# Gate projections of an encoder layer as seven block products instead of eight

## The chip, the cores and the metric

One core of one Trainium2 chip runs the whole layer in one launch. The metric is the device time of that launch in microseconds. Engines are named as in the profile: PE (matrix products), PEld (its weight loads), DVE (VectorE), ACT (ScalarE), POOL (GpSimd) and SP (SyncE, which only issues transfers here). PE writes its results to PSUM, in banks of 128 x 512 float32; everything else on chip lies in SBUF rooms ("tiles" out of pools of a fixed number of rooms).

## The reference

One residual layer over x of 1024 tokens x 1024 channels, float32:

```
h = rmsnorm(x, g_mix);  z = h @ w_in               # pool channels | q | k | v
y_pool = pool_mixer(z[:, :512])                    # trailing windows 2, 4, 8, 16, a map per group
y_attn = diff_attention(q, k, v)                   # 8 heads, two softmax maps each
gates  = sigmoid(h @ w_gate + b_gate)              # w_gate is 1024 x 2048
merged = gates[:, :1024] * (y_pool @ w_branch_pool) + gates[:, 1024:] * (y_attn @ w_branch_attn)
x = x + merged @ w_out
x = x + square(relu(rmsnorm(x, g_ffn) @ w_up)) @ w_down
```

The change concerns `h @ w_gate + b_gate` alone.

## The kernel before

Each float32 factor of a product is kept as two rounded digits, hi and lo, and a product of two factors is three matmuls in one PSUM bank, hi·hi, hi·lo and lo·hi (`mm3`, lines 126 to 128). Making digits is `split`: ACT casts src to hi (line 120), and DVE or POOL subtracts, lo = src - hi (line 121). So a 128 x 512 tile of weights costs one ACT and one DVE or POOL instruction before PE can use it.

The activations h stand transposed in `hT`: eight blocks of 128 channels, two halves of 512 tokens (`th`), two digits. Rows of the outputs of gates, pool channels and so on are channels too, so the gates are 16 blocks of 128 channels (`c`) by two token halves.

The order of the work is this. The eight attention heads run first as a software pipeline over (head, 128 tokens): `z` (q, k, v of a head from `hT`), `tk` (transposes), `sc` (scores), `ta` (transposes of the probabilities), `po` (times v). At the end of each head POOL computes one `r` (line 588). All work of the heads comes first in program order, which is priority here: a scheduler writes each engine's order out ahead of time, and what is later in program order fills the gaps. That filling work, in order, is

- the gates: `gate_cols(c)` loads the weights of a channel block in two halves (`fill_w`, rooms `fr`, two of them), makes digits with POOL's subtract (rooms `fw`, four of them), and for each token half issues 24 matmuls into one bank (`fill_proj`), which ACT copies out with the bias (line 730) and stores to `g_dram`. For c under G_Z = 10 the bank is `ps_f`, of which there is one; from 10 on it is in turn two banks of `ps_z`, which the heads' `z` use until they end, and `ps_f`.
- `weight_unit`, four times: POOL makes sums and digits of `w_branch_attn` for a later stage, started after gate steps 2, 4, 6 and 8.
- the pool channels: `pool_group(g)`, four times, 24 matmuls `u` per token half, a chain of sums on DVE, three matmuls `yp`, and a store to `p_dram`. After nine gate steps (G_FIRST) each half of a group is followed by a gate step.

Behind the heads and the gates come `bp` (16 tiles of 12 matmuls, `branch_pool`), in which each bank is multiplied by a gate half (line 210) that `gate_half` has loaded from `g_dram` and put through the sigmoid (line 828); channel blocks 0 to 7 are used here. Then `ba`, the attention's branch, already as seven block products (`ba_step`, 28 steps of 12 matmuls; banks baX and baY); the gate blocks 8 to 15 are used from its second product on. The stage takes 11 rooms of the pool `up` (`ut`) when the heads have left it: two for `t2`, one for `s2`, four for `wa`, four for `wr`. Then `op` (w_out) and the feed-forward part.

## Time and profile before

| | us |
|---|---|
| median of three runs | 1528.98 (1528.79 to 1530.02) |
| the profiled execution, device time | 1529.71 |
| its span in the profile | 1527.6 |
| last `z` matmul starts | 612.7 |
| last gate matmul starts | 696.7 |
| `bp` | 697 to 740.5 |

The page gives busy time by engine, then the span in 40 slices, each digit the busy share in tenths. In a table by stage each row is one stretch of the span: its length, then for each engine the busy us and, as (x...), the instructions; then PE's granted clock, the busy share of the 16 DMA engines, and GB/s. In a group of instructions the two numbers behind the bar are the busy us and the mean ns of one; in an answer on a tile, the three numbers are the least, the median and the greatest duration in ns.

### The profile page before, as it was taken

What the parts mean: (1) busy time and instruction counts of PE and PEld (TensorE: products, weight loads), DVE (VectorE), ACT (ScalarE), POOL (GpSimd) and SP (SyncE); (2) the same over time, 40 slices, a digit from 0 to 9 for tenths busy, and PEclk for the clock granted to TensorE, in tenths of its full rate; (3) what the DMA queues carried; (4) which work ended last, traced back from release to release, by engine and by line L of the source; (5) the groups of instructions that cost most, each with busy time, mean ns of one, the idle gap of its engine ahead of it and who ended that gap; (6) DMA issues with size and microseconds to landing.
All of it is one profiled execution on the core that took longest, in us unless ns stands there. A gap on an engine that the chain in (4) does not pass through costs nothing.

```text
span 1527.6 us, 21675 instructions
## 1 busy us (share of the span) xinstructions
PE 1509.7 (99%) x7441; PEld 1302.0 (85%) x7441; DVE 1048.5 (69%) x2262; ACT 804.7 (53%) x1693; POOL 319.8 (21%) x412
## 2 busy tenths in 40 slices
PE   7999999999999999999999999999999999999998
PEld 6999999999898989888888888888888888888887
DVE  6776668777777777746578559766665668556572
ACT  6665556656565565454464466555555634333331
POOL 6687333335234242312100011000000000000000
PEclk9999999999999999999999999999999999999999
DMA  7253202112112131627365734554433799537750
GB/s 247 100 159 120 76 29 62 51 44 66 43 44 84 49 98 40 223 89 254 120 209 191 248 104 149 169 178 152 148 128 110 274 344 383 170 125 262 228 190 28
DMA packets 171608, 221.07 MB, mean 145 GB/s; under 512 B 10902, under 2 KB 104811, under 8 KB 171499
## 3 DMA queue, kind: packets, MB, share of 16 engines
q1 hardware_dynamic: 154090, 192.39, 38.0%
q10 hardware_dynamic: 17408, 27.30, 4.8%
q8 instruction: 59, 0.97, 0.3%
q14 instruction: 51, 0.41, 0.1%
HBM read 157.76 MB, written 61.90 MB: 144 GB/s over the span
## 4 chain that ended last, share of the span: by engine, by line
PE 95%; DVE 2%; DMA 1%; ACT 1%; SPq 1%; issue 0%; POOL 0%; DVEq 0%
PE z L126 6%; PE z L128 6%; PE z L127 6%; PE Da L126 4%; PE Da L128 4%; PE Da L127 4%; PE g L126 4%; PE g L127 4%; PE g L128 4%; PE Db L126 3%; PE Db L128 3%; PE Db L127 3%; PE X L128 3%; PE X L127 3%; PE X L126 3%; PE sc L484 2%
## 5 line engine op out<-in xcount | busy, mean ns | idle before, releaser
L126 PE MATMUL z<-wqkv,hT 128*128 128x384 f32 x512 | 174.9, 343 | 0.6 <-DVE qn L428 0.4
L128 PE MATMUL z<-wqkv,hT 128*128 128x384 f32 x512 | 173.7, 340 | 0.0
L127 PE MATMUL z<-wqkv,hT 128*128 128x384 f32 x512 | 173.5, 339 | 0.0
L495 ACT ACTIVATE s<-s,nm 128x256 f32<-128x256 f32 (+7 forms) x128 | 99.5, 778 | 46.5 <-DVE nm L487 45.6
L126 PE MATMUL g<-hT,fwgate 128*128 128x512 f32 x256 | 101.1, 395 | 0.1
L127 PE MATMUL g<-hT,fwgate 128*128 128x512 f32 x256 | 100.8, 394 | 0.0
L128 PE MATMUL g<-hT,fwgate 128*128 128x512 f32 x256 | 100.5, 393 | 0.0
L126 PEld LDWEIGHTS z<-wqkv,hT 128*128 128x128 f32 x512 | 96.8, 189 | 3.4 <-DVE qn L428 0.6
L127 PEld LDWEIGHTS z<-wqkv,hT 128*128 128x128 f32 x512 | 96.9, 189 | 3.1 <-POOL wqkv L121 0.2
L235 POOL TENSOR_TENSOR ms<-ms,mhalf 128x4 f32<-128x4 f32 x64 | 65.7, 1027 | 158.3 <-DVE ms L234 135.3
L128 PEld LDWEIGHTS z<-wqkv,hT 128*128 128x128 f32 x512 | 96.5, 189 | 2.5 <-DVE hT L121 0.3
L121 DVE TENSOR_TENSOR AT<-ta,AT 128x256 fp32r<-128x256 f32 (+1 forms) x160 | 62.2, 392 | 32.7 <-ACT AT L120 31.6
L487 DVE CUSTOM_DVE_ANT_0 s<-sc,dist 128x512 f32<-128x512 f32 (+3 forms) x128 | 73.9, 583 | 13.2 <-PE sc L485 12.1
L120 ACT CAST AT<-ta 128x256 fp32r<-128x256 f32 (+1 forms) x160 | 54.5, 347 | 37.9 <-PE ta L527 23.1
L484 PE MATMUL sc<-K,Q 128*128 128x512 f32 (+2 forms) x192 | 69.8, 365 | 0.5 <-DVE nm L487 0.5
L121 DVE TENSOR_TENSOR AS<-s,AS 128x512 fp32r<-128x512 f32 x64 | 44.1, 693 | 36.5 <-ACT AS L120 36.3
L485 PE MATMUL sc<-K,Q 128*128 128x512 f32 (+2 forms) x192 | 66.4, 350 | 0.0
L121 POOL TENSOR_TENSOR wqkv<-rqkv,wqkv 128x384 fp32r<-128x384 f32 x60 | 61.8, 1044 | 19.8 <-ACT wqkv L120 16.7
L121 POOL TENSOR_TENSOR fwgate<-frgate,fwgate 128x512 fp32r<-128x512 f32 x32 | 43.3, 1356 | 66.0 <-ACT fwgate L120 66.0
L126 PEld LDWEIGHTS g<-hT,fwgate 128*128 128x128 f32 x256 | 48.1, 188 | 9.3 <-ACT go L730 0.5
L128 PEld LDWEIGHTS g<-hT,fwgate 128*128 128x128 f32 x256 | 48.1, 188 | 8.9
L127 PEld LDWEIGHTS g<-hT,fwgate 128*128 128x128 f32 x256 | 48.1, 188 | 8.4
(455 smaller groups left out, 4485.0 us busy)
## 6 DMA issues: line engine op xcount, KB each, us to landing
wd<-in_w_down_dram SPq DMA_DIRECT2D x56, 512.0 KB, 5.6
wu<-in_w_up_dram SPq DMA_DIRECT2D x32, 512.0 KB, 4.4
udS<-us SPq DMA_DIRECT2D x64, 256.0 KB, 2.4
ur<-udS SPq DMA_DIRECT2D x32, 512.0 KB, 3.4
rqkv<-in_w_in_dram SPq DMA_DIRECT2D x64, 192.0 KB, 2.7
ud<-u ACTq DMA_DIRECT2D x48, 256.0 KB, 4.1
ur<-ud SPq DMA_DIRECT2D x24, 512.0 KB, 4.3
frgate<-in_w_gate_dram SPq DMA_DIRECT2D x32, 256.0 KB, 2.8
```

The lines of the kernel that those rows point to most:

```text
L120: nc.scalar.copy(hi, src)
L121: return (lo_eng or nc.vector).tensor_tensor(lo, src, f(hi), op=ALU.subtract)
L126: nc.tensor.matmul(ps, lhs_hi, rhs_hi, start=first, stop=False, **kw)
L127: nc.tensor.matmul(ps, lhs_hi, rhs_lo, start=False, stop=False, **kw)
L128: nc.tensor.matmul(ps, lhs_lo, rhs_hi, start=False, stop=last, **kw)
L235: nc.gpsimd.tensor_tensor(dst, dst, mhalf[:, :n], op=ALU.pow)
L484: nc.tensor.matmul(dst, Q[:, i, 0, :], rhs, start=True, stop=False)
L485: nc.tensor.matmul(dst, Q[:, i, 1, :], rhs, start=False, stop=True)
L487: nc.vector.tensor_tensor_reduce(out=s[i][:, c : c + w], in0=sc[:, 0:w], in1=dist[:, o0 + c : o0 + c + w], scale=2.0 ** -(h + 1), scalar=B ...
L495: nc.scalar.activation(s[i][:, 0:n], s[i][:, 0:n], AF.Exp, bias=last, scale=-1.0, accum_out=Z[:, i, t : t + 1])
```

## The change

With h^T as 2 x 2 blocks (upper and lower 512 input channels, first and second 512 tokens) and w_gate's columns taken in eight groups q of two neighbouring channel blocks, the eight block products of a group become seven (Strassen's scheme in Winograd's form). Each block product is 12 matmuls, so a group issues 84 where it issued 96. Four of the seven need a sum of weight blocks, and four a sum of blocks of `hT`, called T. T takes four 128-channel pieces of two digits: two `fw` rooms, the `fu` room and the `mx` room. It is made four times in turn, in place: t1, t2, t4, t3. Each product or pair of products in one bank is written to a new DRAM tensor `gm_dram` (`spill`), and `sum_gates(q)` reads six of them back into three `ut` rooms, adds five times on POOL, and stores three quarters of the result to `g_dram`; the fourth quarter goes there straight from `first_gate`.

`combine` and the lo subtract are POOL's, except between `late.append(True)` and `late.clear()`, where they are DVE's, weights' digits lie in `wt` rooms (those of the heads' weights), raw weights alternate between the pools `raw` and `fr`, and their loads are issued behind the last load of the heads' weights.

```diff
-PREP_AT = (2, 4, 6, 8)
...
-G_FIRST, G_Z = 9, 10
+G_FIRST = 4
...
-    def gate_cols(c):
-        ws = fill_w(w_gate, c * P, f"gate{c}")
-        for th in range(2):
-            ps = fill_proj(ws, th, f"g{c}_{th}", spare_bank if c >= G_Z else fill_bank)
-            fo = fo_tile(f"go{c}_{th}")
-            nc.scalar.activation(fo[:, 0:512], ps, AF.Identity, bias=cols[:, c : c + 1])
-            nc.scalar.dma_start(g_dram[c * P : (c + 1) * P, th * 512 : (th + 1) * 512], fo[:, 0:512])
-            yield
-
-    def gates():
-        for c in range(2 * NK - 2):
-            yield from gate_cols(c)
-        for gen in [gate_cols(c) for c in (2 * NK - 2, 2 * NK - 1)] * 2:
-            next(gen)
-            yield
+    gm_dram = dram.tile([NK * P, 6 * 512], F32, name="gm_dram")
+    T = {}
+
+    def spill(ps, q, slot, name, m=None, scale=1.0):
+
+        fo = fo_tile(name)
+        if m is None:
+            nc.scalar.copy(fo[:, 0:512], ps)
+        else:
+            c = 2 * q + m
+            nc.scalar.activation(fo[:, 0:512], ps, AF.Identity, bias=cols[:, c : c + 1], scale=scale)
+        if slot is None:
+            dst = g_dram[2 * q * P : (2 * q + 1) * P, 0:512]
+        else:
+            dst = gm_dram[q * P : (q + 1) * P, slot * 512 : (slot + 1) * 512]
+        nc.scalar.dma_start(dst, fo[:, 0:512])
+
+    def raw_gate(dst, q, kh, m):
+        c0 = (2 * q + m) * P
+        nc.sync.dma_start(
+            dst, w_gate[kh * 512 : (kh + 1) * 512, c0 : c0 + P].rearrange("(kk p) c -> p kk c", p=P)
+        )
+
+    def raw_one(q, kh, m, name):
+        if not late:
+            rw = fr_tile([P, 4, P], name)
+            raw_gate(rw, q, kh, m)
+            return rw
+        nraw[0] += 1
+        rw = raw([P, 4, P], name) if nraw[0] % 2 else fr_tile([P, 4, P], name)
+        with tc.issue_after(loaded["wqkv"]):
+            raw_gate(rw, q, kh, m)
+        return rw
+
+    late = []
+    nraw = [0]
+
+    def combine(out, a, b_, op):
+        (nc.vector if late else nc.gpsimd).tensor_tensor(out, a, b_, op=op)
+
+    def digits_of(src, name):
+        w = (wt if late else fw_tile)([P, 2, 4, P], name)
+        stored["lo"] = split(w[:, 0], w[:, 1], src, None if late else nc.gpsimd).ins
+        return w
+
+    def hd(kt, kh, th):
+
+        k = 4 * kh + kt
+        return [hT[k // 2, th, d][:, k % 2, :] for d in range(2)]
+
+    def td(kt):
+        return [T[kt][:, d, :] for d in range(2)]
+
+    def make_T(kt, a, b_, name):
+
+        if kt not in T:
+            if kt < 2:
+                T[kt] = fw_tile([P, 2, 512], f"T{kt}")
+            elif kt == 2:
+                T[kt] = fu_tile("T2").bitcast(F32R).rearrange("p (a b) -> p a b", a=2)
+            else:
+                T[kt] = fq.tile([P, 2, 512], F32R, tag="mx", name="T3")
+        t = T[kt]
+        d = fo_tile(f"{name}_{kt}")[:, 0:512]
+        combine(d, f(a[0]), f(b_[0]), ALU.subtract)
+        combine(d, d, f(a[1]), ALU.add)
+        combine(d, d, f(b_[1]), ALU.subtract)
+        split(t[:, 0, :], t[:, 1, :], d, None if late else nc.gpsimd)
+
+    def product(ps, w, rhs, more=False):
+
+        for kt in range(4):
+            r_hi, r_lo = rhs(kt)
+            mm3(ps, w[:, 0, kt, :], w[:, 1, kt, :], r_hi, r_lo, not more and kt == 0, kt == 3, more)
+
+    def gate_bank(name, spare):
+        return (spare_bank if spare else fill_bank)(name)
+
+    def first_gate(q, spare=False):
+
+        ws = [digits_of(raw_one(q, j, 0, f"gw{j + 1}_{q}"), f"gw{j + 1}_{q}") for j in range(2)]
+        ps = gate_bank(f"gP1_{q}", spare)
+        product(ps, ws[0], lambda kt: hd(kt, 0, 0))
+        spill(ps, q, 0, f"gs1_{q}")
+        product(ps, ws[1], lambda kt: hd(kt, 1, 0), True)
+        spill(ps, q, None, f"gs2_{q}", 0)
+
+    def second_gate(q, spare=False):
+
+        a21, a22 = raw_one(q, 0, 1, f"gw5_{q}"), raw_one(q, 1, 1, f"gx5_{q}")
+        combine(a22, a22, a21, ALU.add)
+        w5 = digits_of(a22, f"gw5_{q}")
+        a11 = raw_one(q, 0, 0, f"gy5_{q}")
+        combine(a11, a11, a22, ALU.subtract)
+        a12 = raw_one(q, 1, 0, f"gz5_{q}")
+        combine(a12, a12, a11, ALU.add)
+        w3 = digits_of(a12, f"gw3_{q}")
+        ps = gate_bank(f"gP5_{q}", spare)
+        product(ps, w5, td)
+        spill(ps, q, 5, f"gs5_{q}", 1)
+        product(ps, w3, lambda kt: hd(kt, 1, 1), True)
+        spill(ps, q, 2, f"gs3_{q}", 0)
+
+    def third_gate(q, spare=False):
+
+        a21, a22 = raw_one(q, 0, 1, f"gx6_{q}"), raw_one(q, 1, 1, f"gy6_{q}")
+        combine(a22, a22, a21, ALU.add)
+        a11 = raw_one(q, 0, 0, f"gz6_{q}")
+        combine(a22, a22, a11, ALU.subtract)
+        ps = gate_bank(f"gP6_{q}", spare)
+        product(ps, digits_of(a22, f"gw6_{q}"), td)
+        spill(ps, q, 1, f"gs6_{q}")
+
+    def fourth_gate(q, spare=False):
+
+        ps = gate_bank(f"gP4_{q}", spare)
+        product(ps, digits_of(raw_one(q, 1, 1, f"gz4_{q}"), f"gw4_{q}"), td)
+        spill(ps, q, 4, f"gs4_{q}", 1, -1.0)
+
+    def fifth_gate(q, spare=False):
+
+        a11, a21 = raw_one(q, 0, 0, f"gx7_{q}"), raw_one(q, 0, 1, f"gy7_{q}")
+        combine(a21, a11, a21, ALU.subtract)
+        ps = gate_bank(f"gP7_{q}", spare)
+        product(ps, digits_of(a21, f"gw7_{q}"), td)
+        spill(ps, q, 3, f"gs7_{q}")
+
+    def sum_gates(q):
+
+        c0, c1, c2 = (ut([P, 2, 512], F32, f"gc{i}_{q}") for i in range(3))
+        for i, c in enumerate((c0, c1, c2)):
+            nc.sync.dma_start(c, gm_dram[q * P : (q + 1) * P, i * 1024 : (i + 1) * 1024])
+        u_, e6, b53, e7, p4, e5 = (c[:, i, :] for c in (c0, c1, c2) for i in range(2))
+        combine(u_, u_, e6, ALU.add)
+        combine(b53, b53, u_, ALU.add)
+        combine(u_, u_, e7, ALU.add)
+        combine(p4, u_, p4, ALU.add)
+        combine(e5, u_, e5, ALU.add)
+        for m, th, c in ((0, 1, b53), (1, 0, p4), (1, 1, e5)):
+            r0 = (2 * q + m) * P
+            nc.sync.dma_start(g_dram[r0 : r0 + P, th * 512 : (th + 1) * 512], c)
...
-    gate_units = gates()
-    steps = [0]
     units_left = [(kk, ch) for kk in range(2) for ch in range(2)]
-
-    def gate_step():
-        more = next(gate_units, "end") != "end"
-        steps[0] += 1
-        if steps[0] in PREP_AT:
-            prepare_weights()
-        return more
 
     def prepare_weights():
         with tc.issue_after(stored["lo"]):
             weight_unit(w_branch_attn, wa_dram, *units_left.pop(0))
 
-    for _ in range(G_FIRST):
-        gate_step()
+    for q in range(G_FIRST):
+        first_gate(q)
+        prepare_weights()
     for g in range(4):
         for _ in pool_group(g):
-            gate_step()
-    while gate_step():
-        pass
+            pass
+    for kt in range(4):
+        make_T(kt, hd(kt, 0, 1), hd(kt, 0, 0), "t1")
+    for q in range(NK):
+        second_gate(q)
+    for kt in range(4):
+        make_T(kt, hd(kt, 1, 1), td(kt), "t2")
+    for q in range(NK):
+        third_gate(q)
+    late.append(True)
+    first_gate(4, True)
+    first_gate(5, True)
+    for kt in range(4):
+        make_T(kt, td(kt), hd(kt, 1, 0), "t4")
+    for q in range(NK):
+        fourth_gate(q, True)
+    first_gate(6, True)
+    for kt in range(4):
+        make_T(kt, hd(kt, 1, 1), hd(kt, 0, 1), "t3")
+    for q in range(NK):
+        fifth_gate(q, True)
+    first_gate(7, True)
+    late.clear()
+    for q in range(NK):
+        sum_gates(q)
     assert not units_left
 
     vpool = attn.enter_context(tc.tile_pool(name="vpool", bufs=1))
```

6 lines of the change are left out of this document (3 added, 3 removed).

## Prediction

> **What bounds the kernel now.** I read the page first: the busy shares, the slices, the chain of work that ended last.
>
> ```profile
> span 1527.6 us, 21675 instructions
> PE 1509.7 (99%) x7441; PEld 1302.0 (85%) x7441; DVE 1048.5 (69%) x2262; ACT 804.7 (53%) x1693; POOL 319.8 (21%) x412
> ...
> GB/s 247 100 159 120 76 29 62 51 44 66 43 44 84 49 98 40 223 89 254 120 209 191 248 104 149 169 178 152 148 128 110 274 344 383 170 125 262 228 190 28
> ...
> PE 95%; DVE 2%; DMA 1%; ACT 1%; SPq 1%; issue 0%; POOL 0%; DVEq 0%
> ```
>
> PE is busy almost without a gap and is 95% of the chain, so a matmul less is worth its time wherever PE stays fed. The next view is the table by stage: start, heads, tail (heads without `z`, with the last gates), `bp`, first part of `ba`.
>
> ```profile
> core 0: us, PE busy (x) PEld busy (x) DVE busy (x) ACT busy (x) POOL busy (x), PEclk, DMA share, GB/s
> ...
> 138.50:612.80 474.30, 473.21 (x2649) 432.33 (x2648) 358.42 (x1108) 278.43 (x750) 179.65 (x217) 1.00 0.19 60
> 612.80:697.00 84.20, 84.20 (x411) 70.15 (x410) 48.32 (x127) 43.02 (x94) 19.54 (x17) 1.00 0.44 152
> 697.00:740.50 43.50, 43.50 (x194) 35.91 (x193) 30.87 (x45) 18.66 (x31) 9.68 (x4) 1.00 0.74 261
> 740.50:770.00 29.50, 29.50 (x132) 24.43 (x131) 17.02 (x27) 13.19 (x23) 0.00 (x0) 1.00 0.29 93
> ```
>
> PE is full in all four at full clock. In the heads DVE is 76% busy, POOL 38%; in the tail POOL is nearly free; under `bp` DVE is at 71% and the transfers at 261 GB/s. The same table for the gate matmuls alone, and for `bp`:
>
> ```profile
> 138.50:612.80 474.30, 91.74 (x357) 1.00 0.19 60
> 612.80:697.00 84.20, 71.23 (x288) 1.00 0.44 152
> ...
> 697.00:740.50 43.50, 43.50 (x192) 1.00 0.74 261
> ```
>
> 288 gate matmuls fill the tail. `bp` is undisturbed 512-column work: 43.5 / 192 = 0.2266 us a matmul, which is how I price one (the durations near 390 ns overlap).
>
> **The change, part by part.** *PE.* 8 groups x (96 - 84) = 96 matmuls go: 96 x 0.2266 = 21.8 us, if PE stays fed. Nothing is added on PE. By the order written, 384 gate matmuls (first_gate of four groups, second, third) use the one filling bank during the heads, against 480 before, and 288 remain for the tail, as many as before. So the gain has to come from shorter heads.
>
> *Do the heads shorten?* The ends of the heads (POOL's `r`) cut the span into head periods; these are the first, the longest and the two shortest of six, for everything, then their gate matmuls, then `u`:
>
> ```profile
> 138.50:219.10 80.60, 80.45 (x447) 73.06 (x446) 53.62 (x173) 44.50 (x120) 30.07 (x37) 1.00 0.19 60
> 219.10:294.30 75.20, 75.20 (x428) 69.28 (x428) 61.86 (x187) 46.22 (x126) 27.83 (x34) 1.00 0.16 51
> 455.60:538.60 83.00, 82.52 (x461) 75.28 (x460) 65.95 (x198) 48.35 (x130) 34.62 (x45) 1.00 0.19 61
> 538.60:612.30 73.70, 73.25 (x415) 66.91 (x414) 55.22 (x174) 43.28 (x119) 25.82 (x29) 1.00 0.24 77
> ...
> 138.50:219.10 80.60, 23.75 (x93) 1.00 0.19 60
> 219.10:294.30 75.20, 12.27 (x48) 1.00 0.16 51
> 455.60:538.60 83.00, 11.59 (x48) 1.00 0.19 61
> 538.60:612.30 73.70, 18.95 (x72) 1.00 0.24 77
> ...
> 138.50:219.10 80.60, 4.51 (x18) 1.00 0.19 60
> 219.10:294.30 75.20, 7.90 (x30) 1.00 0.16 51
> 455.60:538.60 83.00, 12.61 (x48) 1.00 0.19 61
> ```
>
> With 78, 96 and 72 filling matmuls the last three periods shown are 75.2, 83.0 and 73.7 us: fewer fillers, shorter head, at PE's price or faster. The first, with 111, took only 80.6, and over all six periods (fillers 111, 78, 77, 116, 96, 72) the fitted slope is 0.128 us per matmul. So the early loss is between 0 and 96 x (0.2266 - 0.128) = 9.5 us.
>
> It has three places. The pool groups now follow one another with no gate step between, and `yp` waits for a DVE chain. t2 may only overwrite T when the last second_gate product has read it: 16 POOL instructions, some 21 us with little else to fill. And each head's weights come at its very start, load, ACT, then eight subtracts on POOL:
>
> ```profile
> 225.00 10.33 SPq L309 DMA_DIRECT2D rqkv<-in_w_in_dram  x8
> ...
> L121 POOL TENSOR_TENSOR wqkv<-rqkv,wqkv x60: 1003/1015/1470, 9.1 to 546.5; 128x384 fp32r<-128x384 f32 x60
> ```
>
> On SP the a11 and a12 loads of second_gate wait for POOL's sums, and these eight loads can stand behind them; a sum ahead of a subtract costs 1.3 us. Fillers cover that where there are any. I take 5, the middle, since nothing ranks the six periods.
>
> *POOL in the heads.* Lo subtracts: 32 for weights and 8 for t1 and t2, against 20; sums: 40 of weights and 24 for T. That is 84 more, at
>
> ```profile
> L121 POOL TENSOR_TENSOR fwgate<-frgate,fwgate x32: 1278/1292/2191, 26.1 to 672.7; 128x512 fp32r<-128x512 f32 x32
> ...
> L121 POOL TENSOR_TENSOR wbp<-rbp,wbp x8: 1283/1300/4980, 608.9 to 728.3; 128x512 fp32r<-128x512 f32 x8
> ...
> 723.38 6.68 POOL L121 TENSOR_TENSOR wbp<-rbp,wbp 128x512 fp32r<-128x512 f32 x2 [8.08 <-ACT wbp L120]
> ```
>
> 1.292 us: 109 us on POOL's 180 in 474, so about 61%. The heads' own `ms` and `qn` queue behind them for 1.3 us at a time; two `z` banks cover that. second_gate is a chain of three sums and two subtracts on POOL, 6.5 us, with three rounds of loads of 2.8 us: about 15 us for 24 matmuls, where the heads took 24 fillers in some 20 us. Hidden, just.
>
> *ACT* gains 24 hi casts for weights, 16 for T and 24 copies out:
>
> ```profile
> L730 ACT ACTIVATE go<-g,cols 128x512 f32<-128x512 f32 x32 | 21.9, 688 | 15.1 <-PE g L128 13.6 <-DVE cols L372 1.4
> L120 ACT CAST fwgate<-frgate 128x512 fp32r<-128x512 f32 x32 | 19.8, 618 | 12.1 <-PE g L128 10.9 <-DMA frgate<-in_w_gate_dram 1.0 <-ACT oq L560 0.2
> ...
> L121 POOL TENSOR_TENSOR wbp<-rbp,wbp 128x512 fp32r<-128x512 f32 x8 | 14.8, 1865 | 27.7 <-ACT wbp L120 27.7
> ```
>
> 41 us over the heads and tail, in which it is busy 321 of 558. Hidden; if not, a bank comes free 0.7 us late.
>
> *The tail.* DVE gets 24 lo subtracts of weights, 8 sums for P7 and 2 x 16 instructions for t4 and t3:
>
> ```profile
> L199 DVE SCALAR_TENSOR_TENSOR ry<-ry,gs,rb x8: 1269/1285/1502, 613.6 to 714.9; 128x1024 f32<-128x1024 f32 x8
> L846 DVE TENSOR_TENSOR ry<-ry,ry x4: 666/678/1789, 633.5 to 716.9; 128x512 f32<-128x512 f32 x4
> ...
> L210 DVE TENSOR_TENSOR mp<-bp,g x16: 674/683/692, 700.0 to 740.8; 128x512 f32<-128x512 f32 x16
> ```
>
> 64 x 0.683 = 43.7 us on 48.3 that stand there: 92 us of work in 84. About 10 us of it (six L199, two L846) prepares `ba` and may slip. First_gate of 4 and 5 (48 matmuls, 10.9 us) covers t4's 10.9 us of DVE; first_gate of 6 covers half of t3's. Bounds: 0, if the slipping is free, and 7.8 + 10.9 = 19, if PE waits for the excess and for one T. I take 4: half of the excess, as the slipping work has until `ba`.
>
> *The sums behind it.* P7 of group 0 is followed by 7 x 12 + 24 matmuls, 24.5 us. Copy out (0.7), store (2.0), read (4.8) come first, so POOL starts about 17 us ahead of `bp`.
>
> ```profile
> frgate<-in_w_gate_dram SPq DMA_DIRECT2D x32, 256.0 KB, 2.8
> g_dram<-go ACTq DMA_DIRECT2D x32, 256.0 KB, 2.0
> g<-g_dram SPq DMA_DIRECT2D x32, 256.0 KB, 4.2
> ...
> wr<-in_w_branch_attn_dram SPq DMA_DIRECT2D x4, 512.0 KB, 4.8
> ```
>
> The gate halves themselves are in time: `bp` needs a group every 10.9 us, and eight banks let PE run ahead. The rooms are tighter. The sums hold three of eleven `ut` rooms at a time, and `t2`, `s2`, `wa`, `wr` want all eleven; the fourth step of `ba` (51.7 us after `bp` begins) needs `wr` 3, hence its room 6 us before: 63 us after POOL starts. POOL has six other subtracts there. With groups 0 to 5 out of the way (36 instructions) at the 1.865 us that `wbp` averaged (row above): 67 us, 4.5 us late. Bounds: at 1.292 nothing; all 46 at 1.865, 86 us, 23 late. I take 4.5, since the last groups are needed late and `wr` 6 and 7 can wait.
>
> Transfers there: 12.6 MB read and 6.3 MB stored by the sums. Up to 65 us behind `bp`'s start, groups 0 to 5 move 14.2 MB beside some 16.7 MB of old traffic (the stage rows: 152 x 22, 261 x 43.5, 93 x 21.5): 31 MB in 87 us, 355 GB/s, against 383 in the best slice. Full, but not over.
>
> POOL's pace is the weak point: one `wbp` took 4.98 us against 1.28, at 723 to 728, while DVE ran sums of two SBUF tiles without a pause. [...]
>
> *Sum.* -21.8 + 5 + 4 + 4.5 = -8.3 on the profiled execution's 1529.7 (its span is 1527.6, 2.1 lie around it): 1521.4. The median of the runs is 0.7 lower: 1521 rounded.
>
> **The rivals.** *All hidden.* Heads at PE's pace, DVE's excess slipping, sums at 1.3 us: 1529 - 21.8 = 1507. For it: PE has 18 us of gaps in all now (1527.6 less 1509.7). Against: three resources near full at once.
>
> *The sums hold up `ba`* (the other side). POOL at `wbp`'s mean over all 46 instructions, and rooms given to the sums first: PE waits 23 us for `wr` 3; with 5 and 4, 1529 - 21.8 + 32 = 1539. It decides from a mean of 63 / 46 = 1.36 us if all eight groups come first, 1.74 if six. For it: the row of 4.98; the sums also meet t3's and P7's DVE work. Against: POOL's median is 1.30 even so.
>
> *The tail is DVE's.* The whole 19 us, with 5 early and nothing behind: 1529 - 21.8 + 24 = 1531, no change. For it: 92 us in 84. Against: 10 us of it can wait.
>
> **How the numbers follow.** A measurement here tells 0.2% from nothing, 3 us. Forecast, 1512 to 1526: 0.45. All hidden, below 1512: 0.14. No change, 1526 to 1532: 0.13. Slower, the sums: 0.28, of which a third beyond 1541. Faster is 0.59. Range 1507 to 1541: under a tenth above, and a few hundredths below.
>
> **What would show it.** Gate matmuls 672 instead of 768; head periods some 2 to 3 us shorter on average; `z` ending near 596; `bp` beginning near 684 (697 less 21.8, plus 9). If `bp` begins there and PE has gaps behind it with POOL sums of 2 us and more, the bridge decided. If PE has gaps between 320 and 600, the early supply did. Wrong altogether if the head periods stay, or if SP stands in front of a store of the sums with `bp`'s loads behind it.

## The result, and the profile after

The changed kernel takes 1610.99 us (median; 1608.45 to 1611.44) against 1529.28 before: 1.053 times as long, with an interval from 1.051 to 1.055. The forecast was 1521, faster. The profiled execution has a span of 1609.5 us. First the page of the changed kernel: the busy times, the clock and the GB/s by slice (40.2 us each), and the shares of the chain that ended last.

```profile
span 1609.5 us, 22010 instructions
PE 1527.5 (95%) x7345; PEld 1300.6 (81%) x7345; DVE 1103.9 (69%) x2326; ACT 839.5 (52%) x1757; POOL 473.6 (29%) x524
...
PEclk9999999999999899986899999999999999999999
...
GB/s 241 144 148 121 35 57 32 72 21 112 92 138 86 72 91 159 105 183 416 403 210 204 216 211 95 182 159 164 170 131 118 157 360 359 257 128 214 240 206 26
...
PE 74%; DMA 9%; DVE 8%; ACT 2%; issue 2%; POOL 2%; SPq 1%; ACTq 0%; POOLq 0%; DVEq 0%
```

The 96 matmuls are gone, yet PE is busy 17.8 us longer, because matmuls at a lower clock are longer: a gate matmul takes 0.39 us in the median, and up to 0.80 us where the clock stands at 0.50. PE's gaps grew from 17.9 to 82.0 us. Two neighbouring slices carry 416 and 403 GB/s, where the best one before had 383. Now the stages of both kernels: up to the last `z`, from there to the end of `bp`, and in the changed kernel all that follows.

```profile
0.00:612.80 612.80, 601.08 (x3368) 550.14 (x3369) 461.72 (x1411) 361.84 (x974) 275.48 (x372) 1.00 0.26 83
612.80:740.50 127.70, 127.70 (x603) 106.06 (x602) 79.19 (x172) 61.68 (x125) 29.22 (x21) 1.00 0.54 189
```

```profile
0.00:627.90 627.90, 591.73 (x3260) 535.78 (x3261) 466.69 (x1413) 377.29 (x1003) 380.90 (x450) 0.98 0.32 99
627.90:818.90 191.00, 152.85 (x615) 117.70 (x613) 122.17 (x222) 77.73 (x154) 76.43 (x54) 0.85 0.75 274
...
818.90:1609.50 790.60, 782.93 (x3474) 647.17 (x3472) 515.02 (x693) 384.51 (x600) 16.32 (x20) 1.00 0.56 188
```

The first fence is the kernel before, the second the changed one (columns as in the prediction's tables; behind each busy time the number of instructions). The loss of 81.9 us of span is 15.1 ahead of the last `z`, 63.3 between it and the end of `bp`, and 3.5 behind (790.6 against 1527.6 - 740.5 = 787.1).

*Heads.* Before, 3368 matmuls took 612.8 us, 0.182 us each. At that pace the 3260 of the changed kernel would have ended at 593. They end at 627.9: 35 us lost, of which 24.5 are gaps (36.2 against 11.7). The rest is clock: four stretches at half clock, 20.5 us together, to which 10.2 is put down (the last section has them). Of the 108 matmuls that are missing there, 96 are the saving; the rest moved into the tail. Where the gaps lie, by 100 us:

```profile
100.00:200.00 100.00, 94.24 (x524) 85.48 (x523) 76.45 (x236) 56.75 (x153) 54.09 (x76) 0.98 0.29 91
...
300.00:400.00 100.00, 93.82 (x512) 84.16 (x512) 80.44 (x233) 62.02 (x165) 69.42 (x74) 0.98 0.23 71
...
500.00:600.00 100.00, 90.32 (x481) 81.43 (x479) 70.47 (x208) 57.38 (x149) 67.54 (x62) 0.93 0.25 78
```

These are the row of pool groups (100 to 200), the making of t1 (340 to 360) and of t2 (525 to 564). The waits of PE in the heads (what waited, for what; us in total, times, longest) say whose latency shows:

```profile
PE z L127 <- POOL wqkv L121: 3.6, 2, 2.8
PE po L549 <- DVE AT L121: 3.2, 1, 3.2
PE tk L446 <- DVE AT L121: 2.8, 1, 2.8
```

PE does not wait for a gate operand here. It waits for steps of the head's own chain (and 1.3 us for a pool group's `yp`), which fillers covered before. In the kernel before the same list, from 138.5 to the last `z`, has these two entries and no other:

```profile
PE sc L484 <- DVE nm L487: 0.5, 1, 0.5
PE z L126 <- DVE qn L428: 0.4, 1, 0.4
```

What POOL did around the wait of 2.8 us, on its timeline:

```profile
545.40 1.28 POOL L763 TENSOR_TENSOR gy<-gy,gz 128x512 f32<-128x512 f32 x1
546.65 1.25 POOL L121 TENSOR_TENSOR T<-t,T 128x512 fp32r<-128x512 f32 x1
547.87 1.18 POOL L121 TENSOR_TENSOR wqkv<-rqkv,wqkv 128x384 fp32r<-128x384 f32 x1
...
549.43 1.26 POOL L763 TENSOR_TENSOR t<-t,hT 128x512 f32<-128x512 f32 x1
550.66 1.01 POOL L235 TENSOR_TENSOR ms<-ms,mhalf 128x4 f32<-128x4 f32 x1
551.65 0.99 POOL L121 TENSOR_TENSOR wqkv<-rqkv,wqkv 128x384 fp32r<-128x384 f32 x1
```

A sum of weights, a subtract and a sum of T (3.8 us) stand among the head's own `wqkv`, `qn` and `ms`; PE waits for the last row.

*Tail and bp.* 28 MB more go through this stretch: 274 x 191.0 = 52.3 MB, against 189 x 127.7 = 24.1. Of these, 18.9 are the sums (12.6 read, 6.3 stored). The other 9 are, by the program's count, weight loads and partial products of the gate products that follow the last `z`, which the prediction's sum of traffic did not hold (the run without sums still moves 219 x 155.1 = 34.0 MB in this stretch). The stretch from 720 to 810:

```profile
720.00:770.00 50.00, 29.31 (x97) 21.28 (x96) 12.69 (x11) 10.07 (x19) 37.09 (x28) 0.69 1.03 406
770.00:810.00 40.00, 33.71 (x129) 26.42 (x128) 28.78 (x26) 10.79 (x18) 30.16 (x20) 0.87 1.04 401
```

All transfer engines are busy throughout (a share of 1.03 and 1.04), and PE stands still 41% of the first 50 us. Four pieces of the chain that ended last, and the waits of PE behind the last `z`:

```profile
724.53 8.96 DMA ry<-y_dram
...
733.51 8.55 DMA gc<-gm_dram
...
742.12 7.48 DMA g_dram<-gc
...
749.67 8.44 DMA rypT<-p_dram
```

```profile
PE bp L126 <- ACT gs L732: 9.8, 1, 9.8
PE bp L126 <- ACT wbp L120: 5.6, 1, 5.6
PE gP L126 <- ACT gs L732: 5.1, 1, 5.1
PE gP L126 <- ACT T L120: 4.5, 3, 2.5
```

These transfers take 7.5 to 9.0 us, those of the sums (`gc`, `g_dram`) as well as those for `bp` (`ry`, `rypT`). `bp`'s weights (`wbp`) and rows come late, and the longest wait, 9.8 us, is for a copy out (`gs`) of a gate bank on ACT. ACT's timeline ahead of it:

```profile
737.51 0.57 ACT L732 COPY gs<-gP 128x512 f32<-128x512 f32 x1
753.37 0.33 ACTq L740 DMA_DIRECT2D gm_dram<-gs  x1
753.74 0.58 ACT L732 COPY gs<-gP 128x512 f32<-128x512 f32 x1 [15.65 <-DMA rypT<-p_dram]
```

ACT stands 15.3 us between a copy and the issue of the store that belongs to it, and the profile names the landing of a load that SP had issued. The trace shows the pattern: the 807 transfers of the program take eight semaphores in turn, whichever engine issues them, and from 720 to 800 us 68 of 79 are issued within 0.15 us after the transfer that had the same semaphore last has landed. In the kernel before, none of 33 is from 690 to 740. So in this stretch most transfers (those 68 of 79) go out when one of eight in flight comes back, and ACT, which has one to issue, stands still until then: its store at 753.37 goes out 0.08 us after that load, which had the same semaphore, has landed.

### The profile page after: what moved, and what is told of

Same layout as the page of the kernel before. It is cut to its first block, busy times and chain, and to the rows that moved or that the text cites. A ratio compares the mean times of both kernels' runs of the same rounds, so it can differ in the third digit from the quotient of the medians.

```text
span 1609.5 us, 22010 instructions
## 1 busy us (share of the span) xinstructions
PE 1527.5 (95%) x7345; PEld 1300.6 (81%) x7345; DVE 1103.9 (69%) x2326; ACT 839.5 (52%) x1757; POOL 473.6 (29%) x524
## 4 chain that ended last, share of the span: by engine, by line
PE 74%; DMA 9%; DVE 8%; ACT 2%; issue 2%; POOL 2%; SPq 1%; ACTq 0%; POOLq 0%; DVEq 0%
PE z L126 4%; PE z L127 4%; PE z L128 4%; PE Da L126 4%; PE Da L128 4%; PE Da L127 4%; PE Db L128 3%; PE Db L126 3%; PE Db L127 3%; PE X L128 2%; PE X L126 2%; PE X L127 2%; PE gP L127 2%; PE gP L128 2%; PE gP L126 2%
## 5 line engine op out<-in xcount | busy, mean ns | idle before, releaser
L495 ACT ACTIVATE s<-s,nm 128x256 f32<-128x256 f32 (+7 forms) x128 | 99.5, 778 | 35.9 <-DVE nm L487 33.8
L127 PEld LDWEIGHTS z<-wqkv,hT 128*128 128x128 f32 x512 | 98.0, 192 | 7.1 <-POOL wqkv L121 4.7
L126 PEld LDWEIGHTS z<-wqkv,hT 128*128 128x128 f32 x512 | 98.0, 192 | 6.1 <-DVE qn L428 2.6
L128 PEld LDWEIGHTS z<-wqkv,hT 128*128 128x128 f32 x512 | 97.7, 191 | 2.7 <-DVE hT L121 1.1
L235 POOL TENSOR_TENSOR ms<-ms,mhalf 128x4 f32<-128x4 f32 x64 | 69.2, 1081 | 65.7 <-DVE ms L234 58.6
L126 PE MATMUL gP<-T,gw 128*128 128x512 f32 x128 | 50.6, 418 | 4.5 <-ACT T L120 4.5
L127 PE MATMUL gP<-T,gw 128*128 128x512 f32 x128 | 53.1, 415 | 1.6 <-DVE T L121 1.6
L549 PE MATMUL po<-AT,V 128*128 128x512 f32 x128 | 50.4, 411 | 3.2 <-DVE AT L121 3.2
L1229 POOL TENSOR_SCALAR nrs<-nss 128x1 f32<-128x1 f32 x8 | 4.0, 497 | 168.1 <-ACT nsq L1225 168.1
L128 PE MATMUL gP<-T,gw 128*128 128x512 f32 x128 | 52.5, 410 | 0.0
L763 POOL TENSOR_TENSOR gc<-gc,gc 128x512 f32<-128x512 f32 x32 | 47.7, 1502 | 9.8 <-DMA gc<-gm_dram 8.4
L126 PE MATMUL op<-wo,mT 128*128 128x512 f32 x128 | 50.6, 395 | 0.0
```

The source lines that it names most:

```text
L126: nc.tensor.matmul(ps, lhs_hi, rhs_hi, start=first, stop=False, **kw)
L127: nc.tensor.matmul(ps, lhs_hi, rhs_lo, start=False, stop=False, **kw)
L128: nc.tensor.matmul(ps, lhs_lo, rhs_hi, start=False, stop=last, **kw)
L235: nc.gpsimd.tensor_tensor(dst, dst, mhalf[:, :n], op=ALU.pow)
L495: nc.scalar.activation(s[i][:, 0:n], s[i][:, 0:n], AF.Exp, bias=last, scale=-1.0, accum_out=Z[:, i, t : t + 1])
L549: nc.tensor.matmul(both, v_hi, a, start=i == 0, stop=False)
```

## The experiments

All times are medians of the timed runs, beside the kernel before (1528.7 to 1529.8). Timed runs of one kernel lie up to 6 us apart, and most kernels have two or three of them, so a step under some 4 us is not told from none. "Gate by z" is the gate matmuls ahead of the last `z`.

| kernel | us | last z | gate by z | end of bp |
|---|---|---|---|---|
| before | 1529.3 | 612.8 | 480 of 768 | 740.5 |
| b96_half_columns | 1520.1 | 606.4 | 408 of 672 | 730.1 |
| d2_more_early | 1515.3 | 617.2 | 504 of 672 | 725.9 |
| h1_pools_in_a_row | 1550.7 | 629.9 | 455 of 768 | 762.3 |
| changed | 1611.0 | 627.9 | 372 of 672 | 818.9 |
| a2_no_adds | 1609.0 | 624.3 | 372 | 815.9 |
| s1_sums_beside | 1606.0 | 624.5 | 372 | 816.0 |
| d1_half_sums | 1592.5 | 624.8 | 372 | 801.0 |
| a1_no_sums | 1573.5 | 626.7 | 372 | 781.8 |
| a4_no_late_T | 1568.1 | 626.7 | 372 | 774.2 |
| e1_no_T | 1550.0 | 619.3 | 384 | 755.4 |
| w1_weight_sums_on_DVE | 1560.9 | 628.0 | 384 | 762.6 |
| w2_sums_behind_split | 1558.5 | 622.7 | 372 | 765.4 |
| e2_no_T_no_weight_sums | 1534.2 | 602.4 | 384 | 739.7 |
| e3_first_between_too | 1530.4 | 616.7 | 432 | 740.0 |
| c1_first_between | 1638.3 | 617.2 | 386 | 849.0 |
| v1_cover_T | 1658.7 | 617.7 | 336 | 863.9 |
| v2_spread_first | 1625.7 | 618.0 | 324 | 833.6 |

**What 96 matmuls fewer are worth alone.** In the kernel before, four gate columns get half their depth.

```
-            ps = fill_proj(ws, th, f"g{c}_{th}", spare_bank if c >= G_Z else fill_bank)
+            ps = fill_proj(ws, th, f"g{c}_{th}", spare_bank if c >= G_Z else fill_bank, 4 if 2 <= c < 6 else NK)
```

> The kernel before, with the gate products of columns blocks 2 to 5 cut to the first 4 of 8 input blocks: 96 matmuls fewer among the fillers of the heads, everything else (loads, digits, copies out, order) as it was; four column blocks of the gates are so only half computed. If the heads go at PE's pace (my prediction's step), the last z matmul starts 22 us earlier than 612.7, near 591, and the time is near 1507. If the heads have a floor of their own and fillers only use gaps, z ends within 5 us of 612.7, PE shows gaps in the heads, and the time is 1522 to 1529.

Measured 1520.1 us, ratio 0.993 (0.991 to 0.996): 9.7 us instead of 21.8, between the two theories. From 500 to 600 us, for everything and then for the gate matmuls on PE alone:

```profile
500.00:600.00 100.00, 93.45 (x531) 84.69 (x530) 75.26 (x255) 58.01 (x165) 29.02 (x35) 0.98 0.10 32
```

```profile
500.00:600.00 100.00, 7.21 (x27) 0.98 0.10 32
```

27 gate matmuls are left for 100 us that had 93 before, and 6.5 us of gaps open. So the next run gives the filling bank 480 again:

```
-G_FIRST, G_Z = 9, 10
+G_FIRST, G_Z = 9, 12
```

> The kernel before with gate columns 2 to 5 of half the depth (96 matmuls fewer, as measured at 1520.1 us), and the first twelve columns instead of ten in the one filling bank, so that 480 gate matmuls are for the heads, as in the kernel before, and 192 for the tail instead of 288. Theory: the 96 matmuls gave 9.7 us instead of 21.8 because the heads ran out of fillers (500 to 600 us showed 6.5 us of gaps, where the kernel before has 0.5): with the heads full the whole 21.8 comes, 1506 to 1511. Rival: the heads have a pace of their own, and fillers beside them are worth 0.10 us each: 1517 to 1522.

1515.3 us, ratio 0.990 (0.987 to 0.993): 14.4 us, more than the rival and less than the theory. Up to 617.2 the heads run at the old pace (3396 matmuls, 0.182 us each). The rest is lost behind the gates, as the last stages and PE's longest wait there show:

```profile
617.20:669.30 52.10, 52.10 (x258) 43.33 (x257) 42.05 (x100) 30.24 (x69) 11.26 (x10) 1.00 0.59 204
669.30:725.90 56.60, 50.96 (x223) 40.64 (x221) 34.13 (x61) 21.16 (x39) 7.50 (x6) 0.97 0.47 163
```

```profile
PE po L570 <- ACT oqs L120: 4.2, 1, 4.2
```

With 168 gate matmuls in the tail instead of 288, the gates end before the last head's own chain does, and PE waits for it (`po`, 4.2 us). So even with no added work, and in the better of the two orders tried, this saving gives 14 us and not 22: the last fillers were a cover too.

**The sums.** First without them; three of the partial products go straight to their quarters of the gates.

```
+        elif slot in (2, 4, 5):
+            m_, th_ = {2: (0, 1), 4: (1, 0), 5: (1, 1)}[slot]
+            dst = g_dram[(2 * q + m_) * P : (2 * q + m_ + 1) * P, th_ * 512 : (th_ + 1) * 512]
...
-    for q in range(NK):
-        sum_gates(q)
```

> The changed kernel without sum_gates: three partial products go straight to their quarters of g_dram, so the gates are not the right sums; the 18.9 MB of transfers and the 40 adds on POOL are gone, the spills stay. If the stage behind the heads is held by the sums (by transfers or by POOL), the 80 us that the end of bp came late shrink by 35 to 50 and the time is 1560 to 1576. If it is held by the making of T on DVE and by PE's half clock after gaps, the sums are worth under 15 us and the time is 1596 or more. The last z matmul stays near 628 in both.

1573.5 us: the sums are worth 37.5. Then the reads and stores without POOL's adds:

```
-        combine(u_, u_, e6, ALU.add)
-        combine(b53, b53, u_, ALU.add)
-        combine(u_, u_, e7, ALU.add)
-        combine(p4, u_, p4, ALU.add)
-        combine(e5, u_, e5, ALU.add)
```

> The changed kernel with all the reads and stores of the sums but without their 40 POOL adds (the quarters hold single products). If the transfers hold the stage, it stays within 12 us of the changed kernel: 1600 to 1612. If POOL's adds hold it, it comes near the run without sums, 1560 to 1576.

1609.0 us, 2 below the changed kernel, which is not told from none. So POOL's pace, on which the prediction had built its 4.5 us, is not what the sums cost. Then sums for four groups of eight, the others stored directly:

```
-    for q in range(NK):
+    for q in range(NK // 2):
         sum_gates(q)
```

> The changed kernel with sums for the groups 0 to 3 alone; of groups 4 to 7 three partial products are stored straight into their quarters of the gates, so these quarters do not hold the sums. Without any sum it took 1573.5 us, with all of them and no add on POOL 1609, so the transfers are worth some 37 us. Theory 1, that each sum's 2.36 MB is paid at one price: half of it, 1590 to 1593. Theory 2, that the stage has room for a part and pays only what is over it (12.6 MB read and 6.3 stored, at the 383 to 416 GB/s of the best slices, would be 45 to 49 us, so some 10 us are hidden): the half that goes is the dear half, 1575 to 1587. Theory 3, that it is the place on SP ahead of bp's loads: the four groups that stay are the ones that bp's rows need, so most of it stays, 1598 or more.

1592.5 us, ratio 1.041 (1.036 to 1.045): half the sums cost half, 19 of 37.5 us, as theory 1 says. No part of the 18.9 MB is free. Last, all transfers and adds of the sums stay, but `bp` reads gates that were stored directly, as in the run without sums:

```
-            nc.sync.dma_start(g_dram[r0 : r0 + P, th * 512 : (th + 1) * 512], c)
+            nc.sync.dma_start(gx_dram[r0 : r0 + P, th * 512 : (th + 1) * 512], c)
```

> The changed kernel with the three partial products stored straight into their quarters of the gates, as in the run without sums (1573.5 us), so that these quarters do not hold the sums; and beside it all reads, adds and stores of the sums, on the same queue at the same place, with P7 among what is read, but stored to a place that nobody reads. bp waits for no sum any more. Theory 1, contention: the 18.9 MB fill the queues and the transfer engines in front of bp's own loads, whoever needs them: 1598 to 1612. Theory 2, the round trip: bp waits for the sums' store and read back, each some 8 us: 1573 to 1585.

1606.0 us: theory 1. No gate that `bp` reads waits for a sum in this run, and the sums cost 32 us all the same. Its `bp` stage:

```profile
730.00:816.00 86.00, 59.19 (x208) 44.85 (x206) 53.36 (x52) 23.81 (x39) 58.63 (x39) 0.76 0.99 389
```

389 GB/s for 86 us, at 0.99 of the transfer engines. The round trip that `bp` waits for is at most the 5 us to the changed kernel. Whether SP's order, in which `bp`'s loads stand behind the sums' transfers, the eight transfers in flight or the full engines count for most was not tried apart. The trace shows that the issue at a landing comes with the sums: 70 of 80 transfers are issued so in this run (from 720 to 800), 37 of 58 with half the sums and 11 of 47 without (from 720 to 780).

**T.** Without sums, and without t4 and t3:

```
-    for kt in range(4):
-        make_T(kt, td(kt), hd(kt, 1, 0), "t4")
...
-    for kt in range(4):
-        make_T(kt, hd(kt, 1, 1), hd(kt, 0, 1), "t3")
```

> The changed kernel without sums, and without the two remakes of T behind the heads (t4 and t3, 32 instructions on DVE): the fourth and fifth products use the T that is there. Without sums alone it took 1573.5 us; from the last z to the end of bp it took 155 us against 128 before, with 14 us of PE gaps and some 8 us of half clock in 600 to 750. Theory: PE waits there for T, and the half clock follows the wait: 1549 to 1559. Rival: the two fo rooms and the spills hold PE, whatever T does: 1567 to 1574.

1568.1 us, so 5.4 for both, hardly above what these runs tell apart (1570.6 and 1576.4 against 1569.7 and 1566.4): the rival's range, and about what the prediction had given the tail (4). What remains lies mostly beside `bp`:

```profile
626.70:714.00 87.30, 83.77 (x400) 69.28 (x399) 51.75 (x144) 50.54 (x112) 9.07 (x9) 0.98 0.58 191
714.00:774.20 60.20, 53.62 (x217) 42.92 (x216) 46.99 (x61) 24.51 (x41) 11.36 (x6) 0.91 0.87 316
```

The first row holds 278 of the 300 gate matmuls that are left, in 87 us (before: 288 in 84). The second holds the others, 5.6 us, and `bp`, so some 54.6 us for `bp` instead of 43.5, at 316 GB/s and with 6.6 us of gaps. Then no T at all; with the edit below, the four makings of T go too:

```
     def td(kt):
-        return [T[kt][:, d, :] for d in range(2)]
+        return hd(kt, 0, 1)
```

> The changed kernel without sums, and without T at all: the products that use T read the digits of hT's first rows and second half of columns instead (nothing is made, no room is held). Without sums and late T it took 1568.0 us, with the last z at 626.4: 3260 matmuls lie ahead of that point, which at the pace of the kernel before (3368 in 612.8 us) would take 593, so the heads lose some 34 us. Theory: they lose it where the filling bank waits for T; the gaps of 300 to 400 and 500 to 600 us (15.3 us more than before) and their slow clock (some 7) go: z near 604 to 612, time 1545 to 1554. Rival: it is the sums of weights on POOL (40 instructions) in front of the heads' own: z 621 to 627, time 1562 to 1569.

1550.0 us, 18.1 less, in the range of the theory; but `z` ends only 7.4 us earlier, at 619.3, with 12 more gate matmuls done. So about half of the 18 lies in the heads: 7.4 us, and 2.7 for the 12 matmuls. The other half lies behind: from the last `z` to the end of `bp` it takes 136.1 us instead of 147.5, of which 2.7 are again the 12 matmuls. Without T the rooms `fw`, `fu` and `mx` are free, two of which (`fu`, `mx`) also serve `bp`'s row factors. That the rooms are the reason was not tried by itself.

**The sums of weights.** That run without them:

```
-        combine(a22, a22, a21, ALU.add)
...
-        combine(a11, a11, a22, ALU.subtract)
...
-        combine(a12, a12, a11, ALU.add)
...
-        combine(a22, a22, a21, ALU.add)
...
-        combine(a22, a22, a11, ALU.subtract)
```

> The one before (no sums, no T) also without the sums of weights ahead of the second and third products (5 instructions a group on POOL; the loads stay). Theory: POOL's sums are hidden but for a few us: within 5 us of the one before. Rival: they hold each group's filling: 10 to 25 us below the one before, z below 600.

1534.2 us, 15.8 less: the rival's range, and all of it in the heads (`z` at 602.4, just above the rival's 600, with the same 384 gate matmuls done). From 500 to 600 us, with and then without the sums (the last column but three is POOL's):

```profile
500.00:600.00 100.00, 97.90 (x546) 89.95 (x545) 73.64 (x225) 56.98 (x154) 45.89 (x45) 0.98 0.27 84
```

```profile
500.00:600.00 100.00, 99.56 (x570) 91.80 (x569) 72.01 (x237) 61.06 (x169) 32.52 (x37) 1.00 0.24 76
```

24 matmuls more in the same 100 us. Two runs on the reason, each with the sums back in and without T. On DVE:

```
-        (nc.vector if late else nc.gpsimd).tensor_tensor(out, a, b_, op=op)
+        nc.vector.tensor_tensor(out, a, b_, op=op)
```

> The run without sums and without T (1550.0 us, last z at 619), with the sums of weights on DVE in place of POOL. Without them it was 1534.2 and z 602, so they are worth 16 us. Theory 1, POOL's time: the 40 sums stand in POOL's queue ahead of the heads' weights and statistics; on DVE, at some 0.68 us, they hold less: 1537 to 1544. Theory 2, the length of the chain from load to product, wherever it runs: the five steps and three rounds of loads stay, 1546 to 1552. Theory 3, DVE is the tighter engine in the heads (some 75% busy): 1553 to 1562.

1560.9 us, 11 slower than on POOL: theory 3. And on POOL, but each sum behind the split of its tile:

```
-        combine(a22, a22, a21, ALU.add)
         w5 = digits_of(a22, f"gw5_{q}")
+        combine(a22, a22, a21, ALU.add)
```

> The run without sums and without T (1550.0 us, last z at 619), with each sum of weights on POOL behind the split of the tile that it changes instead of ahead of it: the same 40 sums on POOL, and the same rooms, but no product waits for a sum of its own (the products use unsummed weights). Theory 1, POOL's time and the two rooms that the sums keep: the time stays, 1546 to 1553. Theory 2, the chain from load to product: most of the 16 us goes, 1533 to 1541.

1558.5 us, above both ranges. It does not refute theory 2, because the edit takes only the arithmetic off the products' path. Raw weights have two `fr` rooms, so the load of a12 still waits until the sum ahead of it has read its room, and `w3` is made from that load: SP waits 204 us in all for rooms that a sum frees (89.5, 61.4 and 53.4 for `gy`, `gx` and `gz`), against 99 in e1_no_T and none without the sums. So the sums of weights are worth 15.8 us, and the reason stays open between POOL's time, the two rooms with the chain of loads through them, and SP, on which the heads' own loads stand in the same order.

**The order.** Three orders of the changed kernel, with nothing left out. First the first_gate products of groups 4 to 7 between the halves of the pool groups:

```
     for g in range(4):
         for _ in pool_group(g):
-            pass
+            if nhalf[0] % 2 == 0:
+                first_gate(4 + nhalf[0] // 2)
+            nhalf[0] += 1
...
-    first_gate(4, True)
-    first_gate(5, True)
...
-    first_gate(6, True)
...
-    first_gate(7, True)
```

> The changed kernel with the first_gate products of groups 4 to 7 moved from the tail to between the halves of the pool groups: 480 gate matmuls as fillers in the heads, as before the change, 192 behind. If the heads have a floor and lack fillers, z still ends near 628 (within 6 us), the tail is 10 to 25 us shorter, and the time is 1586 to 1600. If the heads go at PE's pace, z ends 20 us later, near 648, and the time stays at 1605 to 1615.

1638.3 us, 27 slower than the changed kernel; both ranges missed. The heads end 11 us earlier, but with 386 gate matmuls done instead of the 480 that I had counted on. What was laid ahead of `t4` and `t3` as a cover is gone, and the waits behind the last `z` grow:

```profile
PE bp L126 <- ACT wbp L120: 24.8, 3, 19.3
PE gP L126 <- ACT T L120: 18.1, 3, 9.7
```

Second, one or two of the first_gate products ahead of each making of T (the tail's are moved in the same way, one ahead of `t4`, one ahead of `t3`, none behind):

```
-    for q in range(G_FIRST):
+    for q in range(2):
         first_gate(q)
         prepare_weights()
...
+    first_gate(2)
+    first_gate(3)
     for kt in range(4):
         make_T(kt, hd(kt, 0, 1), hd(kt, 0, 0), "t1")
...
+    first_gate(4)
+    first_gate(5)
     for kt in range(4):
         make_T(kt, hd(kt, 1, 1), td(kt), "t2")
```

> The changed kernel with its first_gate products laid where T is made: two at the start, two ahead of t1, two ahead of t2, one ahead of t4, one ahead of t3, none at the end (432 gate matmuls early instead of 384, 240 late). Nothing is left out. Theory: the heads lose time where the filling bank waits for T and the head's own chain lies open, so z ends 8 to 16 us earlier (near 612 to 620 instead of 627.6); the tail keeps its waits for T, and the sums their price: 1592 to 1604. Rival: POOL's added work holds the heads, not the missing fillers: z stays within 4 us of 627.6 and the time within 5 of 1611. Second rival: with one first_gate less in the tail T is less covered, and what the heads gain is lost there: 1605 to 1620 with z near 615.

1658.7 us, the slowest; every range missed. `z` ends at 617.7 as the theory says, but with 336 gate matmuls by then, because the early ones were missing at the start:

```profile
0.00:617.70 617.70, 88.20 (x336) 0.98 0.29 92
617.70:785.00 167.30, 98.54 (x336) 0.84 0.48 156
```

The other 336 take 167 us. An earlier last `z` is no gain when fewer fillers are done by then. Third, three of the four early first_gate products spread between pool halves, the tail left as it was:

```
-    for q in range(G_FIRST):
-        first_gate(q)
-        prepare_weights()
+    first_gate(0)
+    prepare_weights()
...
         for _ in pool_group(g):
+            if nhalf[0] % 2 == 0 and nhalf[0] < 6:
+                first_gate(1 + nhalf[0] // 2)
+                prepare_weights()
```

> The changed kernel in its whole, with one first_gate at the start and the three others of the early four between halves of the pool groups; T, the tail and the sums as they are. In the kernel before, pool groups in a row cost 21 us. Theory: the row costs the changed kernel as much or a little less, as it has idle places elsewhere: 1590 to 1602, with the gaps of 100 to 200 us gone. Rival: what is gained between 100 and 300 is lost at t1 and t2, where fewer fillers stand: within 8 us of 1611.

1625.7 us, again slower and beyond both ranges. The gap of 100 to 200 us closes, and another opens where the pool groups now end and T is not made yet:

```profile
100.00:200.00 100.00, 99.14 (x569) 91.77 (x568) 78.56 (x250) 61.08 (x164) 49.12 (x62) 1.00 0.23 72
300.00:400.00 100.00, 88.36 (x478) 77.16 (x478) 75.56 (x229) 56.35 (x152) 50.19 (x63) 0.98 0.18 57
```

So order was tried where all else is simple. The kernel before, with 96 gate matmuls at the start and the pool groups in a row:

```
-PREP_AT = (2, 4, 6, 8)
+PREP_AT = (1, 2, 3, 4)
...
-G_FIRST, G_Z = 9, 10
+G_FIRST, G_Z = 4, 10
...
         for _ in pool_group(g):
-            gate_step()
+            pass
```

> The kernel before in its whole, but with 96 gate matmuls at the start instead of 216, and then the four pool groups with no gate step between their halves, as the changed kernel has them; the rest of the gates behind. Theory: a row of pool groups is a poor filler (a chain through ACT, DVE and POOL between few matmuls), and the heads' own chain lies open: 1533 to 1540, with gaps of 4 us and more between 100 and 300. Rival: the fillers are only exchanged in time: 1527 to 1531.

1550.7 us, ratio 1.014 (1.009 to 1.018): 21 us lost by order alone (that of the gates, and of the four weight units on POOL, which come earlier with it), more than the theory's 4 to 11. PE has gaps of 2.4, 3.7 and 5.7 us in the three stretches from 100 to 400, where the kernel before has 0.2 in all:

```profile
200.00:300.00 100.00, 96.31 (x517) 85.77 (x516) 75.49 (x223) 56.49 (x154) 34.81 (x49) 0.98 0.17 53
300.00:400.00 100.00, 94.31 (x501) 83.43 (x500) 70.05 (x214) 53.61 (x141) 38.34 (x43) 0.98 0.18 59
```

And the order of the first of these runs (the same edit), on the kernel without sums, T and sums of weights:

> The one before (no sums, no T, no sums of weights) with the first_gate products of groups 4 to 7 between the halves of the pool groups, so that 480 gate matmuls are for the heads and 192 for the tail. That is the order that was 27 us dearer with T and sums in (1638.3 against 1611). Theory: that loss came from T and from the sums being laid bare, and the order itself is good: like the kernel before with 96 matmuls fewer and 480 early (1515.3), plus some us for 16 MB more of weight loads and partial products: 1515 to 1530. Rival: pool groups, or the split into twelves, cost by themselves: 1540 or more.

1530.4 us: 3.8 below the same kernel in the changed order (eight runs against seven), no difference from before (1.0003, 0.999 to 1.002), just above the theory's range. The order that cost 27 us there costs nothing here, so it needs T, the sums or the sums of weights beside it. That it lays them bare fits the waits above, of which the largest growth is that of `bp` for its weights (24.8 us against 5.6). This run is also as far as the split came in the orders tried: without any of the added arithmetic it is no faster than the kernel before, and 15 us behind d2_more_early. Behind these 15 the trace shows 72 gate matmuls fewer by the same last `z` (432 against 504). Why the heads take fewer was not tried; d2_more_early also has 216 gate matmuls ahead of the pool groups where this run has 96, so a part can be order.

## Why the prediction was wrong, step by step

The staircase, each step the difference of two measured times: 96 matmuls fewer, with full heads, -14.4 (d2_more_early); the split into products, with its loads and stores, +15.1 (e3_first_between_too less d2_more_early, a part of which can be order); the changed kernel's order +3.8; sums of weights +15.8; T in the heads, and what it holds behind them, +18.1; T in the tail +5.4; the sums +37.5. Together 1610.6. The steps hold in this order only, as c1_first_between against e3_first_between_too shows.

- *-21.8 for the matmuls.* The price was right while PE stays fed: in d2_more_early the heads keep their pace of 0.182 us a matmul. The proviso failed at the end of the last head. Measured -14.4.
- *Heads: +5 (bounds 0 and 9.5).* This step failed. Measured 35 at the old pace; from the prediction's own 591 (612.8 less 21.8) to 627.9 it is 37. The step priced only fillers that are missing from a full supply, by a slope through six periods of 72 to 116 fillers that hardly fix one. What the runs show in its place is the added work: by the same measure the heads lose 24 us without T and 8 without T and the sums of weights, with 384 gate matmuls done by the last `z` in both, so between these two the count of fillers is not the reason. Order counts as well: h1_pools_in_a_row loses 21 us with nothing added. Of the three places that the prediction named, the row of pool groups and t2 are places of gaps; the third, weights behind POOL, shows as two waits of 3.6 us in all, the longer of them inside t2's stretch; and t1, which it did not name, has a gap of 3.2 us.
- *POOL in the heads: hidden.* This term was put at nothing, and it failed. The share of 61% came out close (58%: 283 us of 489 behind 138.5), but a share says nothing of who stands in front or of what comes late: the sums of weights alone are worth 15.8 us, and the half of T's 18.1 that lies in the heads comes on top. The reason behind the 15.8 stays open, as said above.
- *Tail: +4.* What it was meant for, t4 and t3, measured 5.4, so the term was about right, as far as these runs tell. But the stretch from the last `z` to the end of `bp` grew by 63.3 us: 35.9 of it go with the sums (155.1 us are left of 191.0), 7.6 with t4 and t3 (147.5), 11.4 with the rest of T and 12 gate matmuls (136.1), and 8.4 stay against the 127.7 of before. The 9 MB of weights and partial products, which were no term of the sum, move in this stretch too; no run takes them away alone, so their share of the 8.4 is open.
- *Sums: +4.5 (bounds 0 and 23).* The largest error, and the step that failed most: the wait that counts. The prediction looked at POOL's pace (1.865 us a sum) and at the rooms of `ba`. Of the transfers it said "Full, but not over", on 31 MB spread evenly over 87 us. They come at once: one sum stands alone at 682, and all others start behind 724, when the last kind of product (the one with t3) lands, beside `bp`'s own loads. Measured 37.5, by transfers and not by POOL, with 406 GB/s in the worst 50 us.
- *POOL's pace in the sums.* The step took 1.865 us an instruction, `wbp`'s mean. POOL's 40 adds in `sum_gates` averaged 1.47 us, against 1.32 for the 40 sums of weights in the heads: 11% longer, and short of the 1.865. What makes them longer was not tried, and without the adds the time is the same within the noise (1609.0 against 1611.0).
- *The rivals.* The one on the other side had the sums hold up `ba` by POOL's pace: its sign was right, its place and mechanism not. `bp` itself was late. What the prediction had put under "wrong altogether" is what came: the six head periods did not shrink (81.1 us on average, against 79.0), `z` ended at 627.9 and not at 596, and on SP stores of the sums stand between `bp`'s loads.

No run here points to a version of the change that beats the kernel before. A group saves 12 matmuls, 2.7 us at PE's price, and its sum alone costs 37.5 / 8 = 4.7 us in this place.

## What to carry to other kernels

A matmul that fills the gaps of another chain is worth its own time only while another filler is ready; where none is, PE pays the latency that it had covered (96 of them, 21.8 us at PE's price, gave 9.7 and 14.4 here). So list what is ready at each point of the chain, and what its operands wait for, instead of counting fillers over a period. Transfers have to be summed over the stretch in which they can really run, from the moment when their data are there, with the loads of the next stage beside them and every partial product stored on the way (here 406 GB/s in 50 us, where an even spread had given 355); and an engine that issues a store between its own instructions can stand still with it, as ACT does here for 15.3 us. And a share does not say that an engine is free: POOL, at 58% in the heads, had 3.8 us of new work among a head's own, and PE waited 2.8 us for the last of these. Ask whose short instructions will stand behind the new long ones.

## What the hardware showed that was not expected

In this trace the clock falls to half in a gap of 2.8 us, and the prediction had no term for that. PE by single microseconds around the wait of 2.8 us for `wqkv` shown above (busy time, the number of matmuls, clock):

```profile
549.00:550.00 1.00, 0.90 (x4) 1.00 0.00 1
550.00:551.00 1.00, 0.00 (x0) 1.00 0.68 202
551.00:552.00 1.00, 0.00 (x0) 0.86 0.64 191
552.00:553.00 1.00, 0.31 (x1) 0.50 0.00 0
...
558.00:559.00 1.00, 1.00 (x6) 0.72 0.00 0
```

The clock stands at half from 551.7 to 558.6 us, 6.8 us, six of them behind the gap of 2.8 us, so the gap costs about 3 us more than itself (an estimate: at half clock half of the time is lost). In the heads the trace has four such stretches, from 152.4, 360.6, 527.8 and 551.7 us on, of 3.4, 3.4, 6.8 and 6.8 us; half of these 20.5 us, 10.2, is lost by the same estimate, and that is how 24.5 us of gaps became 35. The length of one gap does not decide it here: a gap of 1.44 us at 149.6 (with one of 1.35 us 4 us ahead of it) is followed by a fall, a gap of 1.82 us at 598.3 is not. What does decide it was not tried.

With its 16 transfer engines full (a share of 1.03 and 1.04), this core moved 401 to 406 GB/s over 90 us, above the 383 that I had taken for nearly full.
